# State-space tiles: direct products a tile later, modulation blocks turned by transposes, gelu steps tied behind the scan

## The chip, the cores and the metric

The kernel runs on one core of one Trainium2 chip. The metric is the device time of one execution in microseconds (us); the time before is the median of three runs. The engines are named as the profile names them: PE (TensorE's matmuls), PEld (its weight loads), DVE (VectorE), ACT (ScalarE), POOL (GpSimd) and SP (SyncE, which issues most DMAs).

## The reference

Two decoder layers over one sequence of 256 positions and 2048 channels, all in float32. Each layer has a token mixer and a SwiGLU feed-forward part, each followed by a layer norm with a scaled residual; shifts, scales and gates come from a projection of a conditioning vector. The first layer's mixer, which the change touches, is a state-space model (S5): 128 groups of 16 channels, 64 complex states in each group.

```python
def reference(x, c, ada_w, ada_b, ...):
    c_act = jax.nn.silu(c)
    for i in range(DEPTH):
        mod = c_act @ ada_w[i] + ada_b[i]
        sh_m, sc_m, gt_m, sh_f, sc_f, gt_f = [m[:, None, :] for m in jnp.split(mod, N_MOD, axis=-1)]
        h = x * (1.0 + sc_m) + sh_m
        y = s5_mixer(h, ...) if i % N_MIXERS == 0 else conv_mixer(h, ...)
        x = layer_norm(ALPHA * x + (1.0 + gt_m) * y, ln_g[i, 0], ln_b[i, 0])
        h = x * (1.0 + sc_f) + sh_f
        y = swiglu_ffn(h, ffn_w_gu[i], ffn_w_down[i])
        x = layer_norm(ALPHA * x + (1.0 + gt_f) * y, ln_g[i, 1], ln_b[i, 1])
    return x

def s5_mixer(u, ...):
    ...
    bu = jnp.einsum('btgi,gpi->btgp', u_c.astype(jnp.complex64), b_bar)
    _, h_local = lax.associative_scan(_ssm_combine, (a_elems, bu), axis=1)
    h = h_local + a_pow[None] * h0[:, None]
    y_c = jnp.real(jnp.einsum('btgp,gip->btgi', h, c_mat))
    ...
    y = jax.nn.gelu(y + d_skip.astype(f32) * u.astype(f32)).astype(u.dtype)
    vg = y @ w_glu
    return vg[..., :d] * jax.nn.sigmoid(vg[..., d:])
```

## The kernel before

The state-space part works on 16 tiles of 128 channels (eight groups), all 256 positions at once. Positions are folded in pairs, so that a scan runs over 128 steps. For tile `ct` these steps follow each other:

- `weights_in` copies the input matrices to `mb` (ACT, L396), transposes them on PE into the bank `btr` (L404) and copies that to `lz` (ACT, L405).
- `inputs` transposes x on PE into the bank `xt` (L1333, L1337), and ACT makes from it the modulated inputs `uh` and `u` and the scaled residual `X` (L940, L1345).
- `drive` multiplies `uh` by `lz` into `pin` (PE, L441), a tile of two PSUM banks with two buffers.
- `tables` prepares the rotation table `tab` (ACT L375, POOL L362) and the decay `rho` (ACT, L384).
- `scan` works on DVE: it rotates `pin` (L461, L462, L468, L469), runs one hardware scan over it (L472), and rotates back into `pc` (L461, L462) and `psn` (L459, L462). `pc` and `psn` have one buffer each.
- `weights_out` makes `dd` (the skip on a diagonal, L413) and the output matrices `mc` (L416, L417) on ACT. Nine products on PE (`bdp`, L419 and L423) give the direct block, by which an input acts on the output of its own pair, and ACT copies it to `bd` (four copies, L427).
- `read_out` adds into the bank `y`: the products of `bd` and `dd` with `u` (L484, L485), and those of `mc` with `pc` and `psn` (L495).
- `gelu` takes `y` in three steps: a square on ACT (L1352); a step on DVE (L1355) with a sigmoid on ACT (L1356); and a product on DVE to `gl` (L1360), which is then split into a high part (ACT, L1361) and a low part (POOL, L1362).

These steps are staggered. In iteration `ct` of the loop at L1412, PE issues in this order: `weights_in(ct+1)`, a modulation unit, `read_out(ct-1)`, `inputs(ct+1)`, a modulation unit, `drive(ct+1)`, the nine products of `weights_out(ct+1)`, and the rest of the modulation units. DVE does `scan(ct)` with the gelu steps of tile `ct-1`, each called at one of the places marked `between()`.

Modulation units fill PE's time: each is a DMA of 1 MB of `ada_w` to a buffer `raw` (SP's queue, L583) and four or eight matmuls with the conditioning vector repeated in 32 columns (L627). Four units make a block of 512 columns; its sums lie in the 128 partitions, as four groups of 32 equal rows. ACT copies the block to `adas` (L630). When the next unit is called, the block is first turned (`ada_turn`): four matmuls with a selecting column of `ada_sel` put the totals into columns of a bank `adat` (L635), and one DVE step adds the bias to give `mod` (L637). `plan` sets the units of a tile: 4, 4, 2, 2, then 3 in eight tiles, then 4 in the last four.

What sets the order: in the loop PE's order is the program's (`manual_schedule`). The other engines' instructions are placed by a list scheduler, which works with its own estimate of durations, and each engine then executes in that fixed order. `queue_behind` and `issue_after` add an edge: an instruction is placed on its engine behind another. PSUM banks named `aux` are shared by `btr`, `bdp`, `adat`, `xt` and `y`, three of them. After the loop the last scan and the last gelu run beside the first units of the dense stage (`s5_w_glu`).

Of the kernel before, what the change touches and what calls it, by code (L numbers as in the profile page):

```python
# [11 lines left out]
F32 = mybir.dt.float32  # L12
# [7 lines left out]
P = 128  # L20
# [135 lines left out]
class S5:  # L156
# [250 lines left out]
    def weights_out(self, ct, skip, behind):  # L407

        nc, k = self.nc, ct % 4
        qc, mb, mc = self.qm[ct // 4][1], self.mb[ct % 2], self.mc[ct % 2]  # L410
        dd = self.dd[ct % 2]
        with self.tc.issue_after(behind.ins):
            nc.scalar.mul(dd, self.ident, skip)  # L413
            for par in range(2):
                ps = slice(64 * par, 64 * par + 64)
                nc.scalar.copy(out=mc[ps, 0:4, :, par], in_=qc[ps, :, 4 * k:4 * k + 4])  # L416
                nc.scalar.activation(out=mc[ps, 4:6, :, par], in_=qc[ps, 0:3:2, 4 * k:4 * k + 4], func=AF.Copy, scale=-1.0)  # L417
        bk = self.bank("bdp")
        nc.tensor.matmul(bk[:, 0:32], dd, self.fold, start=True, stop=False)  # L419
        for r_, end in ((0, False), (1, True)):  # L420
            for p in range(4):
                r = slice(32 * p, 32 * p + 32)
                nc.tensor.matmul(  # L423
                    bk[r, 0:32], mb[:, r_, 2 * (p % 2) + p // 2, 1].rearrange("p a b -> p (a b)"), self.cols(ct, r_, p), start=False, stop=end)
        for p in range(4):
            r = slice(32 * p, 32 * p + 32)
            nc.scalar.copy(out=self.bd[ct % 2][r, r], in_=bk[r, 0:32])  # L427
# [16 lines left out]
    def scan(self, ct, pin, tab, between):  # L444

        nc, w = self.nc, self.work
        v = nc.vector
        t, rh = tab

        def turn(out, k):
            o, i = (z.rearrange("p a h r (s c) -> p (a h) r s c", s=2) for z in (out, pin))
            if k == 2:
                for r in range(2):
                    v.scalar_tensor_tensor(out=o[:, :, r, 0], in0=i[:, :, r, 0], scalar=-1.0, in1=t[:, 1, :, ::-1], op0=MUL, op1=MUL)  # L459
            else:  # L460
                v.tensor_tensor(out=o[:, :, :, 0], in0=i[:, :, :, 0], in1=bc(t[:, k, :, ::-1], 2, 2), op=MUL)  # L461
            self.end = v.tensor_tensor(out=o[:, :, :, 1], in0=i[:, :, :, 1], in1=bc(t[:, min(k, 1)], 2, 2), op=MUL)  # L462

        x1 = w.tile([P, 2, 2, 2, HALF], F32, tag="x1", name="x1")
        turn(x1, 0)
        turn(pin, 1)
        xf, pf = (z.rearrange("p a h r (s c) -> p (a h) (r s) c", s=2) for z in (x1, pin))
        v.tensor_tensor(out=pf[:, :, 0::3], in0=xf[:, :, 2:0:-1], in1=pf[:, :, 0::3], op=ADD)  # L468
        v.tensor_tensor(out=pf[:, :, 1:3], in0=xf[:, :, 3::-3], in1=pf[:, :, 1:3], op=SUB)  # L469
        between()  # L470
        z = pin.rearrange("p a h r c -> p (a h r c)")
        v.tensor_tensor_scan(out=z, data0=rh.rearrange("p q r c -> p (q r c)"), data1=z, initial=0.0, op0=MUL, op1=ADD)  # L472
        between()
        pc, psn = (w.tile([P, 2, 2, 2, HALF], F32, tag=n, name=n) for n in ("pc", "psn"))
        turn(pc, 0)
        between()
        turn(psn, 2)
        return pc, psn

# [21 lines left out]
def kernel(  # L501
# [9 lines left out]
    nc = tc.nc  # L511
# [37 lines left out]
        return v.rearrange("a (k p) -> (a k) p", p=P)  # L549

    s5 = S5(tc, const, ident, auxp, "aux", pin_ctx.enter_context(tc.tile_pool(name="pin", bufs=2, space=PSUM)))
    ada_sel = tp.tile([P, 16], F32, name="ada_sel", bufs=1)
    nc.gpsimd.tensor_copy(out=ada_sel, in_=s5.fold[:, 0:16])
    s5_prep = ExitStack()
    s5_pp = s5_prep.enter_context(tc.tile_pool(name="s5prep", bufs=1, side="right"))
    s5.load(s5_pp, s5_lam_re[0], s5_lam_im[0], s5_log_dt)
# [62 lines left out]
    def ada_block(layer, j, c0, n):  # L619

        acc = auxp.tile([P, 512], F32, tag="ada", name="ada", bufs=1)[:, :n]
        kn = 2048 // n
        for u in range(NCH // kn):
            r = load_unit(ada_w[layer], kn * u, kn, [(j * D + c0, n)])
            for k in range(kn):
                kk = kn * u + k
                nc.tensor.matmul(acc[32 * (k % 4):32 * (k % 4) + 32, :], c_rep[:, kk, :], r[:, k, :], start=kk < 4, stop=kk >= NCH - 4)  # L627
            if kk == NCH - 1:
                part = tp.tile([P, 512], F32, tag="adas", name="adas", bufs=1)[:, :n]
                nc.scalar.copy(out=part, in_=acc)  # L630
            yield
        nb, ch = n // P, c0 // P
        tr = aux("adat")[:, :nb]
        for b in range(nb):
            nc.tensor.matmul(tr[:, b:b + 1], part[:, b * P:(b + 1) * P], ada_sel[:, 0:1], start=b == 0, stop=b == nb - 1)  # L635
        with queue_behind([s5.ready]):
            nc.vector.scalar_tensor_tensor(  # L637
                out=mod[layer][:, j, ch:ch + nb], in0=tr, scalar=plus_one(j), in1=ab_col[layer][:, 16 * j + ch:16 * j + ch + nb], op0=ADD, op1=ADD)

    class AdaQueue:  # L640

# [43 lines left out]
        def add(self, layer, j, b0, k, r):  # L685
            nb = 4 - b0
            rows, n = 4 // nb, 512 * nb
            if k == 0:
                self.acc = sp_ada.tile([P, D], F32, tag="adaacc", name="adaacc")
            acc = self.acc[:, :n]  # L690
            for i in range(rows):
                kk = rows * k + i
                if kk == 0:
                    nc.vector.tensor_scalar(out=acc, in0=r[:, 0], scalar1=c_act[:, 0:1], scalar2=None, op0=MUL)
                else:
                    nc.vector.scalar_tensor_tensor(out=acc, in0=r[:, i], scalar=c_act[:, kk:kk + 1], in1=acc, op0=MUL, op1=ADD)  # L696
            if kk < NCH - 1:
                return
            h = 32 * nb

            def total():
                ps = auxp.tile([P, 512], F32, tag="ada", name="adar", bufs=1)
                for b in range(nb):
                    nc.tensor.matmul(ps[32 * b:32 * b + 32, :], ones[:, 0:32], acc[:, 512 * b:512 * b + 512], start=True, stop=True)
                part = tp.tile([P, 512], F32, tag="adas", name="adas", bufs=1)
                nc.scalar.copy(out=part[:h], in_=ps[:h])
                later.put(1, lambda: turned(part))

            def turned(part):
                tr = aux("adat")  # L710
                for b in range(4):
                    nc.tensor.transpose(tr[:, b * h:(b + 1) * h], part[:h, b * P:(b + 1) * P], ident[:h, :h])
                nc.vector.scalar_tensor_tensor(
                    out=mod[layer][:, j, 4 * b0:].rearrange("p (b c) -> p c b", c=4),
                    in0=tr[:, :4 * h].rearrange("p (c b r) -> p c b r", b=nb, r=32)[:, :, :, 0],
                    scalar=plus_one(j), in1=ab_col[layer][:, 16 * j + 4 * b0:16 * j + 16].rearrange("p (b c) -> p c b", c=4),
                    op0=ADD, op1=ADD)

            later.put(1, total)


# [625 lines left out]
    def gelu(ct, u, y):  # L1347

        vv, uu = y, u.rearrange("p (t c) -> p t c", t=2)

        def first():
            nc.scalar.activation(out=uu, in_=vv, func=AF.Square, scale=math.sqrt(0.044715))  # L1352

        def second():
            nc.vector.scalar_tensor_tensor(out=uu, in0=uu, scalar=1.0, in1=vv, op0=ADD, op1=MUL)  # L1355
            nc.scalar.activation(out=uu, in_=uu, func=AF.Sigmoid, scale=GELU_C)  # L1356

        def third():
            g = w.tile([P, SEQ], F32, tag="gl", name="gl", bufs=1)
            last = nc.vector.tensor_tensor(out=g.rearrange("p (t c) -> p t c", t=2), in0=uu, in1=vv, op=MUL)  # L1360
            nc.scalar.copy(out=hh[:, ct], in_=g)  # L1361
            nc.gpsimd.tensor_tensor(out=hl[:, ct], in0=g, in1=hh[:, ct].bitcast(F32), op=SUB)  # L1362
            return last

        return first, second, third
# [23 lines left out]
    def scan(ct, now, y):  # L1389
# [1 line left out]
        nonlocal held  # L1391
        turns = list(gelu(*held[:2], y)) if held else []

        def between():
            if turns:
                turns.pop(0)()

        held = ct, now[1], *s5.scan(ct, now[2], tabs.pop(ct), between)
        while turns:
# [2 lines left out]
    with tc.manual_schedule(engines={mybir.EngineType.PE}):  # L1402
# [9 lines left out]
        for ct in range(NCH - 1):  # L1412
            now, y = coming, None
            if (ct + 1) % 4 == 1 and ct < 12:
                load_x(ct // 4 + 1)
            s5.weights_in(ct + 1)
            n = plan[ct + 1]
            ada_units(n > 0)
            with queue_behind([] if ct else [s5.made]):
# [8 lines left out]
            s5.weights_out(ct + 1, d_col[:, ct + 1:ct + 2], last)  # L1428
            ada_units(n - 2)
            if ct == NCH - 2:  # L1430
                raws[:] = [rawp]
                more.close()
                s5.keep_ctx.close()
# [15 lines left out]
    def s5_end():  # L1449
        y = s5.read_out(*held)  # L1450
        for fn in gelu(*held[:2], y):
            last = fn()
        held_back[:] = [last]
        s5.work_ctx.close()
        s5.mats_ctx.close()
# [318 lines left out]
```

## Time and profile before

| | us |
|---|---|
| median of three runs | 2298.04 (2293.91 to 2303.72) |
| profiled execution, its time | 2298.96 |
| its span, first to last instruction | 2296.8 |
| PE busy (share of the span) | 2237.6 (97%) |
| PEld busy | 1814.5 (79%) |
| DVE busy | 1671.6 (73%) |
| ACT busy | 1019.6 (44%) |
| POOL busy | 157.2 (7%) |
| start of the scan of tile 0 | 43.41 |
| start of the scan of tile 15 | 221.87 |

A line of the timeline gives the start, the length, the engine, the source line, the operation, the tile written and the tiles read, their shapes, and how often it occurs; in brackets stands the idle time of the engine ahead of it and what ended it. PE's matmuls in float32 appear as two records each, transposes as one. A row of waits says who waited for whom, how long in total, how often, and the longest. The columns of a view of windows are the length, the busy time of PE, PEld, DVE, ACT and POOL with the number of records, the mean granted TensorE clock (1.00 is full speed), the busy share of the DMA engines and GB/s. Durations of neighbouring lines on one engine overlap a little, so distances are taken from start to start.

### The profile page before, as it was taken

To read this page: it belongs to the slowest core of one execution; us is meant where nothing else is said; L and a number is where in the kernel's file an instruction comes from. 1 tells how busy PE (TensorE), PEld (TensorE's weight loads), DVE (VectorE), ACT (ScalarE), POOL (GpSimd) and SP (SyncE) were. 2 spreads that over 40 slices of the span, in tenths; PEclk is the share of its full clock that TensorE was granted. 3 is DMA by queue.
4 is the path that set the end of the run, shared out by engine and by line. 5 is a ranking of instruction groups with operands and counts; after the bars stand their busy time and mean duration, and the time that the engine had idled before them with its cause. 6 is when DMAs were issued, how large, how long until landed. Compare 5 with 4: busy or idle time off the path is not lost.

```text
span 2296.8 us, 33538 instructions
## 1 busy us (share of the span) xinstructions
PE 2237.6 (97%) x13683; PEld 1814.5 (79%) x13683; DVE 1671.6 (73%) x1808; ACT 1019.6 (44%) x1237; POOL 157.2 (7%) x266
## 2 busy tenths in 40 slices
PE   7998999999999999999999999999999999999998
PEld 4555877988778887878898776898888888888888
DVE  8787888887777777777989788888755444545474
ACT  5665334654433333334446333656443333344343
POOL 5762000000000000000010110000000000000000
PEclk8999999999999999999999999999999999999999
DMA  9988799588999899899866774766875555555542
GB/s 333 312 288 263 267 337 356 166 307 309 323 321 324 331 317 315 312 309 328 303 209 195 213 209 160 271 218 202 289 234 191 187 192 190 183 192 191 185 166 91
DMA packets 380607, 579.48 MB, mean 252 GB/s; under 512 B 13875, under 2 KB 277939, under 8 KB 365987
## 3 DMA queue, kind: packets, MB, share of 16 engines
q1 hardware_dynamic: 379862, 576.82, 74.2%
q8 instruction: 107, 1.75, 0.3%
q0 software_dynamic: 352, 0.45, 0.1%
q14 instruction: 46, 0.38, 0.1%
q10 hardware_dynamic: 240, 0.08, 0.0%
HBM read 573.72 MB, written 3.57 MB: 251 GB/s over the span
## 4 chain that ended last, share of the span: by engine, by line
PE 80%; DVE 8%; ACT 5%; DMA 5%; issue 2%; POOL 0%; SPq 0%; DVEq 0%; ACTq 0%
PE acc L884 63%; PE acc L888 5%; DMA raw<-in_ffn_w_gu_dram 3%; DVE wlo L829 2%; PE acc L1000 2%; PE turned L900 2%; ACT whi L828 2%; PE ada L627 1%; PE y L495 1%; DMA raw<-in_s_w_glu_dram 1%; PE conv L1665 1%; DVE adaacc L696 1%; PE adat L635 1%; PE xt L1337 0%; ACT uh L940 0%
## 5 line engine op out<-in xcount | busy, mean ns | idle before, releaser
L829 DVE TENSOR_TENSOR wlo<-raw,whi 128x2048 fp32r<-128x2048 f32 x344 | 788.8, 2294 | 461.9 <-ACT whi L828 454.9
L828 ACT CAST whi<-raw 128x2048 fp32r<-128x2048 f32 x344 | 655.5, 1906 | 814.4 <-PE acc L884 426.1
L884 PE MATMUL acc<-whi,h 128*128 128x512 f32 x3648 | 892.0, 393 | 7.3 <-ACT whi L828 7.0
L884 PEld LDWEIGHTS acc<-whi,h 128*128 128x128 f32 x3648 | 679.6, 188 | 161.7 <-ACT whi L828 14.5
L884 PE MATMUL acc<-wlo,h 128*128 128x512 f32 x1824 | 461.4, 390 | 0.5 <-DVE wlo L829 0.4
L884 PEld LDWEIGHTS acc<-wlo,h 128*128 128x128 f32 x1824 | 341.8, 188 | 73.1 <-DVE wlo L829 2.2
L884 PE MATMUL acc<-whi,f 128*128 128x512 f32 x1248 | 300.9, 391 | 0.0
L696 DVE SCALAR_TENSOR_TENSOR adaacc<-rawa,c_act,adaacc 128x2048 f32<-128x2048 f32 (+1 forms) x135 | 284.5, 2107 | 0.4
L884 PEld LDWEIGHTS acc<-whi,f 128*128 128x128 f32 x1248 | 232.8, 188 | 49.5 <-ACT whi L828 1.7
L884 PE MATMUL acc<-wlo,f 128*128 128x512 f32 x624 | 156.4, 389 | 0.0
L884 PEld LDWEIGHTS acc<-wlo,f 128*128 128x128 f32 x624 | 117.1, 188 | 24.3
L1595 POOL TENSOR_TENSOR lw<-fold,wtap 128x1024 f32<-128x1024 f32 x12 | 26.3, 2196 | 1062.1 <-PE acc L888 872.8
L627 PE MATMUL ada<-raw,c_rep 128*32 128x512 f32 (+1 forms) x576 | 76.8, 634 | 2.3 <-POOL qc L324 1.6
L1233 ACT ACTIVATE fsg<-acc 128x256 f32<-128x256 f32 x84 | 31.7, 379 | 98.2 <-PE acc L884 98.2
L888 PE MATMUL acc<-h,whi 128*128 128x256 f32 x512 | 67.3, 286 | 2.8 <-DVE h L1698 2.2
L888 PEld LDWEIGHTS acc<-h,whi 128*128 128x128 f32 x512 | 63.7, 193 | 8.0 <-DVE h L1698 3.1
L1177 POOL CAST lnmh<-lno 128x2 fp32r<-128x2 f32 x1 | 0.2, 181 | 885.2 <-DVE lno L68 885.2
L1234 DVE TENSOR_TENSOR fsg<-acc,fsg 128x256 f32<-128x256 f32 x84 | 35.0, 419 | 17.2 <-ACT fsg L1233 17.2
L1665 PE MATMUL conv<-vs,lw 128*32 128x256 f32 x720 | 42.2, 380 | 0.1
L888 PE MATMUL acc<-f,whi 128*128 128x256 f32 x320 | 40.7, 284 | 0.0
L888 PEld LDWEIGHTS acc<-f,whi 128*128 128x128 f32 x320 | 39.3, 192 | 0.2
L472 DVE TENSOR_TENSOR_SCAN pin<-rho,pin 128x1024 f32<-128x1024 f32 x16 | 36.7, 2292 | 0.4
(349 smaller groups left out, 1859.1 us busy)
## 6 DMA issues: line engine op xcount, KB each, us to landing
raw<-in_ffn_w_gu_dram SPq DMA_DIRECT2D x352, 512.0 KB, 4.7
rawa<-in_ada_w_dram SPq DMA_DIRECT2D x128, 1024.0 KB, 5.6
raw<-in_ffn_w_down_dram SPq DMA_DIRECT2D x88, 1024.0 KB, 5.1
raw<-in_ada_w_dram SPq DMA_DIRECT2D x64, 1024.0 KB, 7.9
raw<-in_s_w_glu_dram SPq DMA_DIRECT2D x64, 512.0 KB, 5.9
raw<-in_cv_w_pw_dram SPq DMA_DIRECT2D x64, 512.0 KB, 5.8
raw<-in_cv_w_pw_dram SPq DMA_DIRECT2D x16, 1024.0 KB, 5.7
vs<-scr SPq DMA_DIRECT2D x40, 142.0 KB, 5.8
```

The costliest lines, as they stand in the source:

```text
L472: v.tensor_tensor_scan(out=z, data0=rh.rearrange("p q r c -> p (q r c)"), data1=z, initial=0.0, op0=MUL, op1=ADD)
L627: nc.tensor.matmul(acc[32 * (k % 4):32 * (k % 4) + 32, :], c_rep[:, kk, :], r[:, k, :], start=kk < 4, stop=kk >= NCH - 4)
L696: nc.vector.scalar_tensor_tensor(out=acc, in0=r[:, i], scalar=c_act[:, kk:kk + 1], in1=acc, op0=MUL, op1=ADD)
L828: m1 = nc.scalar.copy(out=self.hi[:, :kn], in_=r[:, :kn])
L829: m2 = nc.vector.tensor_tensor(out=self.lo[:, :kn], in0=r[:, :kn], in1=self.hi[:, :kn].bitcast(F32), op=SUB)
L884: nc.tensor.matmul(acc[bank].rearrange("p a b -> p (a b)"), x[:, bank * HALF:(bank + 1) * HALF], wt[:, k], start=first, stop=end)
L888: nc.tensor.matmul(acc[bank][:, i], wt[:, k, m * P:(m + 1) * P], x, start=first and i == 0, stop=end and i == 1)
L900: nc.tensor.transpose(b[:, o:o + HALF], u[t][:, c0 + k * P:c0 + (k + 1) * P], ident)
L1000: nc.tensor.matmul(acc[m][:, 0:EW], wt[:, k, m * P:(m + 1) * P], xx[:, 4 * u + k], start=u == 0 and n == 0, stop=u == 3 and n == len(order ...
L1233: nc.scalar.activation(out=t[:, i], in_=gv[:, 0], func=AF.Sigmoid)
L1234: nc.vector.tensor_tensor(out=t[:, i], in0=gv[:, 0], in1=t[:, i], op=MUL)
L1665: nc.tensor.matmul(acc[32 * q:32 * q + 32, :], lw[:, q, g, :], vs[:, q, 4 * g:4 * g + SEQ], start=g == 0, stop=g == n - 1)
```

## The change

Three edits.

- The direct block's nine products and four copies become a method of their own, `direct(ct)`. It is called one iteration later, behind `weights_in(ct+1)`; for tile 0 in iteration 1 ahead of `weights_in(2)`, and for tile 15 at the end of iteration 14. `dd` and `mc` are still made where they were.
- A modulation block is turned by four transposes of 128 by 128 instead of the four products with `ada_sel`, which is dropped. A DVE reduction adds the four rows that count (columns 0, 32, 64 and 96 of each transposed block) and puts the sums in the same PSUM bank; the step to `mod` reads them there. The tile `adas` gets 16 columns more, which nothing uses.
- The DVE steps of gelu get an edge each: the second step (L1355) behind the scan, the third (L1360) behind the last step to `pc`.

```diff
+    def direct(self, ct):
+
+        nc, mb, dd = self.nc, self.mb[ct % 2], self.dd[ct % 2]
         bk = self.bank("bdp")
         nc.tensor.matmul(bk[:, 0:32], dd, self.fold, start=True, stop=False)
...
-        v.tensor_tensor_scan(out=z, data0=rh.rearrange("p q r c -> p (q r c)"), data1=z, initial=0.0, op0=MUL, op1=ADD)
-        between()
+        done = v.tensor_tensor_scan(out=z, data0=rh.rearrange("p q r c -> p (q r c)"), data1=z, initial=0.0, op0=MUL, op1=ADD)
+        between(done)
         pc, psn = (w.tile([P, 2, 2, 2, HALF], F32, tag=n, name=n) for n in ("pc", "psn"))
         turn(pc, 0)
-        between()
+        between(self.end)
         turn(psn, 2)
...
-    ada_sel = tp.tile([P, 16], F32, name="ada_sel", bufs=1)
-    nc.gpsimd.tensor_copy(out=ada_sel, in_=s5.fold[:, 0:16])
...
-                part = tp.tile([P, 512], F32, tag="adas", name="adas", bufs=1)[:, :n]
+                part = tp.tile([P, 528], F32, tag="adas", name="adas", bufs=1)[:, :512][:, :n]
...
-        tr = aux("adat")[:, :nb]
+        tr = aux("adat")
         for b in range(nb):
-            nc.tensor.matmul(tr[:, b:b + 1], part[:, b * P:(b + 1) * P], ada_sel[:, 0:1], start=b == 0, stop=b == nb - 1)
+            nc.tensor.transpose(tr[:, b * P:(b + 1) * P], part[:, b * P:(b + 1) * P], ident)
+        sums = tr[:, 1:1 + nb]
         with queue_behind([s5.ready]):
-            nc.vector.scalar_tensor_tensor(
-                out=mod[layer][:, j, ch:ch + nb], in0=tr, scalar=plus_one(j), in1=ab_col[layer][:, 16 * j + ch:16 * j + ch + nb], op0=ADD, op1=ADD)
+            nc.vector.tensor_reduce(
+                out=sums, in_=tr[:, :n].rearrange("p (b q r) -> p b q r", q=4, r=32)[:, :, :, 0], axis=mybir.AxisListType.X, op=ADD)
+        nc.vector.scalar_tensor_tensor(
+            out=mod[layer][:, j, ch:ch + nb], in0=sums, scalar=plus_one(j), in1=ab_col[layer][:, 16 * j + ch:16 * j + ch + nb], op0=ADD, op1=ADD)
...
-        def second():
-            nc.vector.scalar_tensor_tensor(out=uu, in0=uu, scalar=1.0, in1=vv, op0=ADD, op1=MUL)
+        def second(behind):
+            with queue_behind(behind):
+                nc.vector.scalar_tensor_tensor(out=uu, in0=uu, scalar=1.0, in1=vv, op0=ADD, op1=MUL)
             nc.scalar.activation(out=uu, in_=uu, func=AF.Sigmoid, scale=GELU_C)
 
-        def third():
+        def third(behind):
             g = w.tile([P, SEQ], F32, tag="gl", name="gl", bufs=1)
-            last = nc.vector.tensor_tensor(out=g.rearrange("p (t c) -> p t c", t=2), in0=uu, in1=vv, op=MUL)
+            with queue_behind(behind):
+                last = nc.vector.tensor_tensor(out=g.rearrange("p (t c) -> p t c", t=2), in0=uu, in1=vv, op=MUL)
...
+            if ct == 1:
+                s5.direct(0)
             s5.weights_in(ct + 1)
+            if ct:
+                s5.direct(ct)
             n = plan[ct + 1]
             ada_units(n > 0)
...
             if ct == NCH - 2:
+                s5.direct(ct + 1)
```

More of the change, by code (lines that the diff above doesn't have):

```diff
@@ L409, in weights_out @@
         nc, k = self.nc, ct % 4
-        qc, mb, mc = self.qm[ct // 4][1], self.mb[ct % 2], self.mc[ct % 2]
+        qc, mc = self.qm[ct // 4][1], self.mc[ct % 2]
         dd = self.dd[ct % 2]
@@ L704, in total @@
                     nc.tensor.matmul(ps[32 * b:32 * b + 32, :], ones[:, 0:32], acc[:, 512 * b:512 * b + 512], start=True, stop=True)
-                part = tp.tile([P, 512], F32, tag="adas", name="adas", bufs=1)
+                part = tp.tile([P, 528], F32, tag="adas", name="adas", bufs=1)[:, :512]
                 nc.scalar.copy(out=part[:h], in_=ps[:h])
@@ L1349, in gelu, with first @@
         vv, uu = y, u.rearrange("p (t c) -> p t c", t=2)
-        def first():
+        def first(behind):
             nc.scalar.activation(out=uu, in_=vv, func=AF.Square, scale=math.sqrt(0.044715))
-        def second():
-            nc.vector.scalar_tensor_tensor(out=uu, in0=uu, scalar=1.0, in1=vv, op0=ADD, op1=MUL)
+        def second(behind):
+            with queue_behind(behind):
+                nc.vector.scalar_tensor_tensor(out=uu, in0=uu, scalar=1.0, in1=vv, op0=ADD, op1=MUL)
             nc.scalar.activation(out=uu, in_=uu, func=AF.Sigmoid, scale=GELU_C)
-        def third():
+        def third(behind):
             g = w.tile([P, SEQ], F32, tag="gl", name="gl", bufs=1)
-            last = nc.vector.tensor_tensor(out=g.rearrange("p (t c) -> p t c", t=2), in0=uu, in1=vv, op=MUL)
+            with queue_behind(behind):
+                last = nc.vector.tensor_tensor(out=g.rearrange("p (t c) -> p t c", t=2), in0=uu, in1=vv, op=MUL)
             nc.scalar.copy(out=hh[:, ct], in_=g)
@@ L1392, in scan, with between @@
         turns = list(gelu(*held[:2], y)) if held else []
-        def between():
+        def between(*behind):
             if turns:
-                turns.pop(0)()
+                turns.pop(0)(behind)
         held = ct, now[1], *s5.scan(ct, now[2], tabs.pop(ct), between)
@@ L1451, in s5_end @@
         for fn in gelu(*held[:2], y):
-            last = fn()
+            last = fn(())
         held_back[:] = [last]
```

## The prediction

> **What bounds the kernel now.** The diff touches only the state-space stage, so I first looked for where that stage lies. The scan (L472), one for each of 16 tiles, begins at 43.41 us for tile 0 and at 221.87 us for tile 15. I cut this stretch at the scans' starts in the view of windows (the columns are length, then busy time of PE, PEld, DVE, ACT, POOL, then the granted clock, the DMA share and GB/s), and asked for the waits of DVE and PE over the 13 intervals from scan 2 to scan 15.
>
> ```profile
> 71.84:221.87 150.03, 133.62 (x1961) 80.34 (x1959) 124.61 (x194) 99.83 (x284) 82.55 (x155) 0.92 0.83 280
> ...
> 104.76:116.49 11.73, 10.76 (x156) 6.43 (x152) 9.59 (x15) 7.20 (x22) 10.90 (x27) 0.85 0.91 305
> ...
> 139.86:149.50 9.64, 9.64 (x162) 5.50 (x156) 9.40 (x16) 7.47 (x22) 6.57 (x13) 1.00 0.94 330
> ...
> 195.83:209.15 13.32, 11.91 (x172) 6.83 (x164) 9.74 (x15) 7.05 (x20) 3.54 (x6) 0.88 0.65 220
> ```
>
> 150.03 us for 13 tiles is 11.54 us a tile, and 124.61 us of DVE is 9.59. The tile from 139.86 took 9.64 us with DVE busy for 9.40: a tile can go at VectorE's own pace. Others with the same DVE work take 11.73 or 13.32, at a lower granted clock. So the stage alternates between VectorE and TensorE, and what it loses stands in the waits (us in total, times, longest):
>
> ```profile
> DVE mod L637 <- PE adat L635: 7.2, 7, 1.6
> DVE gl L1360 <- ACT u L1356: 5.8, 7, 1.8
> DVE u L1355 <- ACT u L1352: 5.6, 5, 1.9
> DVE pc L461 <- PE y L495: 2.1, 2, 1.2
> DVE x L461 <- PE pin L441: 1.9, 2, 0.9
> ...
> PE adat L635 <- ACT adas L630: 6.3, 5, 1.6
> PE bdp L423 <- ACT mc L416: 5.5, 11, 0.5
> PE bdp L419 <- ACT dd L413: 1.7, 4, 0.5
> ```
>
> The five DVE rows add up to 22.6 us: DVE without them would need 127.4 us. That is the most the change could take out here. DMA is not the bound: its queue waits for TensorE to give buffers back.
>
> ```profile
> SPq L583 <- PE ada L627: 176.1, 52, 26.0
> ```
>
> The 13 tiles moved 280 GB/s, and the tile from 139.86 moved 330. The same bytes in 137 us need 280 x 150/137 = 307 GB/s, still below that.
>
> **Part 1, gelu steps tied behind the scan.** Nothing is added; two VectorE steps and the sigmoid between them get an order. In the interval from 104.76 VectorE stood still ahead of the first of them, with the scan's last preparation (L469) and the scan behind it:
>
> ```profile
> 112.83 0.69 DVE L468 TENSOR_TENSOR pin<-x,pin 128x512 f32<-128x512 f32 x1
> 115.43 0.42 DVE L1355 SCALAR_TENSOR_TENSOR u<-u,y 128x256 f32<-128x256 f32 x1 [1.90 <-ACT u L1352]
> 115.77 0.69 DVE L469 TENSOR_TENSOR pin<-x,pin 128x512 f32<-128x512 f32 x1
> 116.49 2.29 DVE L472 TENSOR_TENSOR_SCAN pin<-rho,pin 128x1024 f32<-128x1024 f32 x1
> 118.82 0.69 DVE L461 TENSOR_TENSOR pc<-pin,tab 128x512 f32<-128x512 f32 x1
> 119.43 0.68 DVE L462 TENSOR_TENSOR pc<-pin,tab 128x512 f32<-128x512 f32 x1
> 120.03 0.41 DVE L1360 TENSOR_TENSOR gl<-u,y 128x256 f32<-128x256 f32 x1
> ...
> 113.89 1.06 PE L495 MATMUL y<-psn,mc 128*32 128x128 f32 x32
> ```
>
> Behind the scan, the step comes later by L469 (0.72 from start to start) and the scan (2.33): 3.05 us, more than the longest wait of 1.9. So the row of 5.6 us goes whole: -5.6. What is late next is pc, which shares its buffer with the y product; its last records began at 113.89 and took 1.06, so it had ended at 114.95, when pc would start at 118.82 - 1.90 = 116.92 and not wait.
>
> The second step (gl) needs the sigmoid. From L1355's start to gl's place there would be 0.33 for L1355 itself and 1.21 us for the two pc steps; 0.41 plus the sigmoid's 0.42 fits. But ScalarE is in order:
>
> ```profile
> 177.09 0.42 ACT L1356 ACTIVATE u<-u 128x256 f32<-128x256 f32 x1
> 177.42 0.72 ACT L427 COPY bd<-bdp 32x32 f32<-32x32 f32 x4
> ...
> 180.54 0.58 ACT L630 COPY adas<-ada 128x512 f32<-128x512 f32 x1
> ...
> 129.95 0.42 DVE L1360 TENSOR_TENSOR gl<-u,y 128x256 f32<-128x256 f32 x1 [0.72 <-ACT u L1356]
> ...
> 172.90 0.42 DVE L1355 SCALAR_TENSOR_TENSOR u<-u,y 128x256 f32<-128x256 f32 x1 [0.25 <-ACT u L1352]
> ...
> 177.61 0.42 DVE L1360 TENSOR_TENSOR gl<-u,y 128x256 f32<-128x256 f32 x1 [1.83 <-ACT u L1356]
> ...
> 217.88 0.42 DVE L1360 TENSOR_TENSOR gl<-u,y 128x256 f32<-128x256 f32 x1 [0.79 <-ACT u L1356]
> ```
>
> L1355 had run at 172.90, and the sigmoid of that tile came only at 177.09, in its place in ScalarE's order. That order can stay. Bounds of this term: all 5.8 us gone, or the longest wait of 1.83 in all 13 tiles, 23.8 - 5.8 = +18.0. I take -2.3: three waits (the first 0.72 at 129.95, the last 0.79 at 217.88, and another 0.79 between), where gl followed a late L1355 with little between them, and leave the other four to ScalarE's order.
>
> **Part 2, direct blocks at the next tile's beginning.** Moved are nine products (18 records, L419 and L423) on PE and the four copies to bd on ACT; no DMA, and nothing of SP's or POOL's queue. On PE they pass the last modulation units and the transposes to btr; on ACT they leave the place ahead of rho and adas shown above, 0.72 us. Now PE reaches them before mc is there:
>
> ```profile
> 118.74 0.33 PE L423 MATMUL bdp<-mc,mb 128*32 128x32 f32 x16 [0.50 <-ACT mc L416]
> 118.89 1.04 PE L627 MATMUL ada<-raw,c_rep 128*32 128x512 f32 x8
> 119.86 0.66 PE L404 MATMUL btr<-ident,mb 128*128 128x128 f32 x4
> 121.57 1.05 PE L635 MATMUL adat<-ada_sel,adas 128*128 128x1 f32 x8 [1.05 <-ACT adas L630]
> ...
> 106.95 0.33 PE L423 MATMUL bdp<-mc,mb 128*32 128x32 f32 x16 [0.49 <-ACT mc L416]
> ...
> 110.20 1.93 PE L627 MATMUL ada<-raw,c_rep 128*32 128x512 f32 x8
> ...
> 208.24 1.94 PE L627 MATMUL ada<-raw,c_rep 128*32 128x512 f32 x8
> ```
>
> A modulation unit (0.97 us from the start of one at 118.89 to btr at 119.86) and btr later, mc is long written, so the PE waits for dd and mc, 5.5 + 1.7 = 7.2 us, go. Then the direct products (0.33 for L423's eight; two more for L419) stand between btr and the turn of the modulation block and fill part of its wait for adas. PE time alone earns nothing in tiles that VectorE paces; it shortens what VectorE waits for. Two rows do: pc and x, 2.1 + 1.9 = 4.0 us, all in the last two intervals, with four units a tile. Of the tile from 195.83, PE's 0.50 at mc and the low clock go: the unit at 208.24 takes 1.94 against 1.04, 0.9 more. Two such tiles with about 1.4 to 1.5: -3.0 (bounds 0 and -4.0).
>
> The clock is a cost in itself. Some 3 us after the gap of 0.49 us ahead of 106.95, PE's unit at 110.20 took 1.93 instead of 1.04, and the interval from 104.76 has 0.85. The Trainium skill ("TensorE: Matmul & The Clock Gate", Part 1, HAM oscillation) says that the clock drops once PE idles for a whole window of some 3.4 us; by that, removing gaps of half a microsecond would give no clock back, and this term would be 2 x 0.5 = -1.0 rather than -3.0. The trace speaks against it: PE was busy 10.76 of that interval's 11.73 us, so no gap came near 3.4 us, and still the clock fell; the interval with PE busy throughout (from 139.86) stands at 1.00.
>
> **Part 3, the turn by transposes.** Eight records of 1.05 us become four like btr's 0.66, 0.39 less for each of the 10 turns between scans 2 and 15. ScalarE's copy to adas stands up to 0.72 us sooner without the bd copies, so the turn ends about 1 us sooner in the tiles where mod is waited for 1.0 to 1.6 us. VectorE's place for mod isn't fixed by the change, and VectorE too arrives sooner. Bounds of the row of 7.2: gone, or all still there. I take half, -3.6. Added is one reduction for each block, 16 elements in and 4 out of each partition. No such row exists; nearest is mod itself:
>
> ```profile
> 108.31 0.16 DVE L637 SCALAR_TENSOR_TENSOR mod<-adat,adab 128x4 f32<-128x4 f32 x1
> 108.39 0.42 DVE L1360 TENSOR_TENSOR gl<-u,y 128x256 f32<-128x256 f32 x1
> ```
>
> It took 0.08 us from start to start and 0.16 in all. The reduction reads four times its elements; I take the middle, 0.12 x 10 = +1.2 (bounds 0.8 and 1.6). The ada_sel copy on POOL before the stage and the padding of part cost nothing: POOL is busy 82.55 of the 13 tiles' 150.03 us, and the padded columns are never touched.
>
> **Start and end.** From scan 1 to scan 2 y(0) is late, and direct(0) and direct(1) still stand ahead of it, now beside the transposes; their wait for mc goes (0.50 in the row at 118.74), and y(0) gets a wait for bd's copies (0.72 in the row at 177.42): 0, bounds -2 and +2. Behind scan 15 the dense stage is paced by its weights; one turn and the last gelu there: 0.
>
> **Sum**: -5.6 - 2.3 - 3.0 - 3.6 + 1.2 = -13.3 us. The profiled execution took 2298.96 (span 2296.8), 0.92 above the median of 2298.04. 2298.96 - 13.3 = 2285.7; rounded, 2286. The stage would then run at (150.03 - 13.3)/13 = 10.5 us a tile.
>
> **Rivals.**
> *The PSUM bank.* Three banks serve btr, bdp, adat, y and xt; y holds one until gl. The new order puts btr, bdp and adat into one run, while y is held. For it:
>
> ```profile
> 109.19 0.68 PEld L404 LDWEIGHTS btr<-ident,mb 128*128 128x128 f32 x4 [0.84 <-DVE gl L1360]
> 109.19 1.08 PE L404 MATMUL btr<-ident,mb 128*128 128x128 f32 x4
> ```
>
> PE now comes about 1 us sooner to that place, so I estimate the wait at 0.84 to 1.8 us in the ten tiles with a turn. Against it: bank choice isn't in the trace, and PE has room in three-unit tiles. It would eat the terms of mod, pc and x (-6.6): 2292.
>
> *The transposes lower the clock.* As a mechanism of this kernel: each turn brings a slow stretch, costing 0.89 for a unit (1.93 against 1.04) and 0.42 for btr (1.08 against 0.66), 1.3 x 10 = 13 us of PE, partly the stretches it has already. Against it: 139.86 to 149.50, with four transposes, stands at 1.00. The terms of mod, pc and x would go here too: 2292. The same page of the Trainium skill (Part 4, PE-mode transpose) says that transposes don't count as busy for the clock gate, which is this rival; no run here shows it yet.
>
> *ScalarE paces gl; the other side.* If gl, now always directly behind pc, waits in every tile for a sigmoid that stands behind dd and mc, its term is up to +18.0 instead of -2.3, and the sum -11.0 + 18.0 = +7.0: 2306. It is slower than before from an average wait of (11.0 + 5.8)/13 = 1.3 us a tile. Against it: gl's place further back isn't forbidden, and of 13 tiles 7 have a wait now, 5.8/7 = 0.8 us on average.
>
> *All waits go*: -5.6 - 5.8 - 4.0 - 7.2 + 0.8 = -21.8: 2277.
>
> **Chances and range.** Forecast 0.52, bank 0.15, clock 0.10, ScalarE 0.10, all waits 0.13. What a measurement of this kernel can tell from no change is about 0.5%, 11.5 us: the border lies at 2286.5, in the middle of the forecast's own range (2281 to 2293). So faster is 0.13 and a little over half of 0.52, 0.42 in all; same is the rest of the forecast, both middle rivals and the mild half of ScalarE's, 0.52; slower 0.06. The range runs from 2275 to 2300, which leaves out the far end of ScalarE's case and little else.
>
> **What would show it.** Right: L1355 behind every scan with no wait of over 0.3 us ahead of it; bdp without a wait for dd or mc; adat at about 0.66; granted clock near 1.0 in most tiles; 10 to 10.8 us from scan to scan. Wrong: a row of PE waiting for gl or for bd; gl or the new reduction waiting over 0.8 us a tile; intervals of 11.5 us still.

## The result and the profile after

The changed kernel takes 2275.61 us (median of four runs, 2274.40 to 2277.76) against 2295.97 us before (four runs): a ratio of 0.9907, 95% interval 0.9880 to 0.9933. It is 20.4 us faster, where 12 were forecast and the likeliest outcome (0.52) was one that a measurement can't tell from no change; the time lies at the fast end of the range. One of the five executions of the kernel with the turn alone (`turn_only`, below) took 5458.29 us, more than twice the others, and is left out of its ratio.

The gain lies in the state-space stage. The view of windows of the changed kernel, cut at the starts of its scans (now L476) as before: the sum from scan 2 to scan 15, four tiles with three units, then two with four.

```profile
71.86:201.85 129.99, 117.08 (x1903) 71.20 (x1895) 123.99 (x203) 98.69 (x283) 81.13 (x151) 0.98 0.92 320
...
91.11:100.87 9.76, 9.76 (x168) 5.83 (x162) 9.52 (x16) 8.75 (x27) 7.24 (x14) 1.00 1.02 360
...
120.34:130.15 9.81, 9.81 (x172) 6.06 (x168) 9.47 (x14) 8.42 (x25) 6.01 (x11) 1.00 0.86 293
...
139.91:149.68 9.77, 8.02 (x114) 5.28 (x114) 9.53 (x16) 6.08 (x18) 9.22 (x24) 0.83 0.98 347
149.68:160.66 10.98, 10.01 (x178) 6.20 (x173) 9.62 (x17) 8.02 (x23) 7.79 (x13) 1.00 0.78 265
160.66:171.00 10.34, 9.22 (x138) 5.33 (x134) 9.54 (x16) 7.53 (x22) 2.77 (x5) 1.00 0.88 304
...
180.84:191.20 10.36, 9.63 (x160) 5.71 (x160) 9.67 (x17) 6.83 (x20) 2.74 (x5) 1.00 0.93 346
```

The 13 tiles take 129.99 us instead of 150.03, so 20.0 us of the 22.1 by which the spans differ (2274.7 against 2296.8). Scan 2 begins where it did, at 71.86. Tiles with up to three units now run at 9.6 to 9.8 us, but for one of 10.98, with VectorE busy for about 9.5; those with four units need 9.8 to 10.65. The granted clock is 0.98 instead of 0.92. The waits of VectorE and TensorE in the same stretch:

```profile
DVE gl L1367 <- ACT u L1362: 3.1, 4, 1.2
...
PE adat L637 <- ACT adas L632: 5.0, 7, 1.1
...
PE bdp L423 <- DVE mod L642: 1.9, 1, 1.9
PE bdp L423 <- DVE gl L1367: 1.6, 1, 1.6
...
PE bdp L427 <- ACT mc L416: 0.5, 1, 0.5
```

Of VectorE's five rows before (22.6 us) one is left. TensorE's waits for dd and mc fell from 7.2 to 0.5. The waits of bdp for mod and gl are those of the bank rival. The first of them:

```profile
103.07 0.66 PE L404 MATMUL btr<-ident,mb 128*128 128x128 f32 x4
105.63 0.38 PE L423 MATMUL bdp<-fold,dd 128*128 128x32 f32 x2 [1.91 <-DVE mod L642]
...
103.08 0.41 DVE L1361 SCALAR_TENSOR_TENSOR u<-u,y 128x256 f32<-128x256 f32 x1
...
104.92 0.17 DVE L640 TENSOR_REDUCE adat<-adat 128x4 f32<-128x16 f32 x1
105.00 0.41 DVE L463 SCALAR_TENSOR_TENSOR psn<-pin,tab 128x256 f32<-128x256 f32 x1
105.34 0.15 DVE L642 SCALAR_TENSOR_TENSOR mod<-adat,adab 128x4 f32<-128x4 f32 x1
```

PE stood for 1.91 us until mod was written; the trace doesn't name banks, but a bank that adat still held explains it. That tile still took 9.77 us (100.87 to 110.64). The reduction takes 0.17 us, and 0.08 from start to start. The second, in the tile from 139.91, was not free:

```profile
144.51 0.41 PE L423 MATMUL bdp<-fold,dd 128*128 128x32 f32 x2 [1.57 <-DVE gl L1367]
...
146.88 1.94 PE L499 MATMUL y<-pc,mc 128*32 128x128 f32 x32
148.58 1.59 PE L499 MATMUL y<-psn,mc 128*32 128x128 f32 x32
...
154.67 0.42 DVE L1367 TENSOR_TENSOR gl<-u,y 128x256 f32<-128x256 f32 x1 [1.18 <-ACT u L1362]
```

Behind the wait of 1.57 us the clock fell, and the products of y took 1.94 and 1.59 us where they take 1.08 and 1.06 otherwise. ScalarE, which had waited for y, came late to the sigmoid, VectorE waited 1.18 us for it, and that tile is the one of 10.98.

### The profile page after: what moved, and what is told of

It is laid out like the page before. It is cut to its first block, busy times and chain, and to the rows that moved or that the text cites. A ratio compares the mean times of both kernels' runs of the same rounds, so it can differ in the third digit from the quotient of the medians.

```text
span 2274.7 us, 33445 instructions
## 1 busy us (share of the span) xinstructions
PE 2221.7 (98%) x13619; PEld 1804.2 (79%) x13619; DVE 1671.7 (73%) x1826; ACT 1018.8 (45%) x1237; POOL 157.0 (7%) x265
## 4 chain that ended last, share of the span: by engine, by line
PE 79%; DVE 10%; DMA 4%; ACT 4%; issue 2%; SPq 0%; POOL 0%; DVEq 0%; ACTq 0%
PE acc L889 65%; PE acc L893 6%; DVE wlo L834 3%; DMA raw<-in_ffn_w_gu_dram 3%; ACT whi L833 2%; PE acc L1005 2%; PE turned L905 2%; PE conv L1677 1%; DVE adaacc L701 1%; PE y L499 1%; DMA raw<-in_s_w_glu_dram 1%; PE ada L629 1%; DMA raw<-in_ada_w_dram 1%; DVE pin L476 1%; PE adar L709 0%
## 5 line engine op out<-in xcount | busy, mean ns | idle before, releaser
L629 PE MATMUL ada<-raw,c_rep 128*32 128x512 f32 (+1 forms) x576 | 71.3, 592 | 6.0 <-DMA raw<-in_ada_w_dram 3.6
L476 DVE TENSOR_TENSOR_SCAN pin<-rho,pin 128x1024 f32<-128x1024 f32 x16 | 36.7, 2294 | 0.5
```

The lines of the kernel that those rows point to most:

```text
L476: done = v.tensor_tensor_scan(out=z, data0=rh.rearrange("p q r c -> p (q r c)"), data1=z, initial=0.0, op0=MUL, op1=ADD)
```

## The experiments

**Each part alone, and the whole without the direct part.** The edits are the hunks of the diff: `gelu_only` has the ties, `direct_only` the direct method and its calls, `turn_only` the transposes with the reduction, `no_direct` the first and the last of these.

> The kernel before with only the gelu steps tied behind the scan. Theory of separate rows (each part of the change takes out the wait rows that it touches): L1355's row of 5.6 us and 2.3 us of gl's go, about -8 us. Rival of a common cause (TensorE comes late because of its own gaps and the clock that they cost, and every VectorE wait is that lateness seen at another place): the wait only moves to mod, pc or x; -4 us or less, and the granted clock in the 13 tiles stays near 0.92.

> The kernel before with only the direct blocks a tile later. Separate rows: TensorE's waits for dd and mc go, VectorE's waits for pc and x (4.0 us) shrink by 3: -3 us. Common cause: the granted clock rises towards 1.0, TensorE is earlier everywhere, and the rows of mod, L1355, gl, pc and x all shrink: -12 us or more.

> The kernel before with only the modulation blocks turned by transposes. Separate rows: half of mod's row goes and the reduction costs 1.2: -2 to -3 us. Common cause: TensorE's gaps at mc stay, so does the clock; -1 to -4 us. The rival that transposes lower the clock: granted clock below 0.92 in the 13 tiles, 0 or slower.

> The changed kernel with the direct blocks where they were before (gelu tied, turns by transposes). Separate rows: 3 us slower than the changed kernel, so about -17 against before. Common cause: most of the gain is lost, -6 us or less against before, with TensorE's waits for dd and mc and a granted clock near 0.92 back.

Ratios to before: gelu alone 0.9996 (0.9982 to 1.0011); direct alone 0.9942 (0.9918 to 0.9965); turn alone 0.9924 (0.9891 to 0.9956); gelu and turn 0.9924 (0.9899 to 0.9950). In the gelu kernel, VectorE's waits between scans 2 and 15:

```profile
DVE gl L1362 <- ACT u L1357: 9.7, 8, 2.1
DVE mod L637 <- PE adat L635: 8.9, 7, 1.6
DVE pc L461 <- PE y L495: 2.2, 2, 1.2
DVE x L461 <- PE pin L441: 1.9, 2, 0.9
```

L1355's row is gone, as meant, and the sum is 22.7 us, as before: gl has 3.9 more and mod 1.7 more. The wait moved and nothing was gained. The windows of direct alone with VectorE's waits, then those of turn alone with TensorE's waits:

```profile
72.95:209.24 136.29, 125.34 (x1943) 78.63 (x1935) 123.51 (x194) 98.90 (x283) 80.87 (x151) 0.95 0.88 304
...
DVE u L1359 <- ACT u L1356: 4.0, 2, 2.4
DVE gl L1364 <- ACT u L1360: 2.5, 4, 0.8
DVE x L465 <- PE pin L445: 2.2, 3, 0.9
DVE pc L465 <- PE y L499: 1.0, 1, 1.0
```

```profile
70.62:206.62 136.00, 120.28 (x1921) 70.90 (x1919) 124.58 (x203) 99.39 (x284) 82.38 (x156) 0.99 0.91 311
```

```profile
PE bdp L423 <- ACT mc L416: 5.5, 11, 0.5
...
PE bdp L419 <- ACT dd L413: 1.6, 4, 0.5
```

Either part by itself takes 14 us out of the stage. For the direct part the theory of a common cause had said 12 or more; for the turn no theory had said more than 4. The direct part empties mod's row, which it doesn't touch. In turn alone TensorE still stands for dd and mc as long as before, and yet its clock is 0.99. So those gaps by themselves don't lower the clock; with the one-column products beside them it is 0.92, and without the gaps but with the products (direct alone) 0.95. The rival that transposes lower the clock falls. In `no_direct` the theory of separate rows had the right number, -17 us (measured, by the ratio: -17.5). The common cause, as it was written down for that run, failed: the gaps are back, the clock stays at 0.99, and most of the gain stays too.

What 0.92 consists of shows when the kernel before is cut finer. The clock is 0.50 in seven stretches of 3.41 us, whole multiples of 3.41 us apart, and 1.00 between them. One of them, with the stretch ahead of it:

```profile
105.86:109.27 3.41, 2.73 (x35) 1.72 (x36) 3.38 (x7) 3.32 (x12) 3.05 (x11) 1.00 0.91 330
109.28:112.69 3.41, 3.41 (x15) 1.42 (x16) 3.27 (x6) 1.86 (x5) 3.18 (x7) 0.50 0.66 201
...
106.95 0.33 PE L423 MATMUL bdp<-mc,mb 128*32 128x32 f32 x16 [0.49 <-ACT mc L416]
107.22 1.05 PE L635 MATMUL adat<-ada_sel,adas 128*128 128x1 f32 x8
```

Ahead of each of the seven stands such a stretch with gaps of 0.68 to 1.64 us and a turn by one-column products (about 1.05 us) together. In the rest of the stage it stayed at 1.00 behind a turn with gaps of at most 0.22 us (three times), and behind gaps of up to 1.4 us without a turn. Longer gaps did lower it without a turn: 2.6 us at the stage's end are followed by one more such stretch, just outside it. So the seven fall where gaps and turn meet, and either part of the change takes away much of one of them.

**What of the turn counts: how it streams, or how long it takes?** First, the kernel before with 96 selecting columns instead of one (the 32 columns of `fold` three times; only the first of each 96 results is read):

```diff
-    ada_sel = tp.tile([P, 16], F32, name="ada_sel", bufs=1)
...
+    ada_sel = tp.tile([P, 96], F32, name="ada_sel", bufs=1)
+    for q in range(3):
+        nc.gpsimd.tensor_copy(out=ada_sel[:, 32 * q:32 * q + 32], in_=s5.fold)
...
-            nc.tensor.matmul(tr[:, b:b + 1], part[:, b * P:(b + 1) * P], ada_sel[:, 0:1], ...)
+            nc.tensor.matmul(tr[:, b * P:b * P + 96], part[:, b * P:(b + 1) * P], ada_sel, ...)
```

Then the changed kernel with products added behind the transposes, one column wide or 128:

```diff
+        for b in range(nb if layer == 0 and (j, c0) != (3, 512) else 0):
+            nc.tensor.matmul(acc[:, b:b + 1], part[:, b * P:(b + 1) * P], ident[:, 0:1], start=True, stop=True)
```

```diff
+        for b in range(nb if layer == 0 and (j, c0) != (3, 512) else 0):
+            nc.tensor.matmul(acc[:, 0:P], part[:, b * P:(b + 1) * P], ident, start=True, stop=True)
```

> The kernel before, its turn still by products with the selecting column, but with that column repeated to 96, so that each product streams 96 columns instead of 1 (the same count of records, no transposes, no reduction on VectorE, PE's turn not shorter than 1.05 us). Theory N: the one-column products leave TensorE idle in the eyes of its clock, and the low clock (0.92 in the 13 tiles) is what the transposes took away; then the clock rises to 0.97 or more here too and the time falls by 10 us or more. Rival S (shorter): the transposes gain because they take 0.66 us instead of 1.05; then this kernel is as slow as before, within 3 us. Rival O (order): the reduction gave VectorE's two steps another place; then this kernel is as slow as before too.

> The changed kernel with, behind each turn's transposes, the one-column products of before again, into a bank that nothing reads any more (11 of 12 blocks; no result changes). Theory N: the clock falls back under 0.95 and 8 us or more of the gain is lost. Rival S: TensorE has room beside VectorE, 1.0 us more a turn costs at most the tiles with four units, 0 to 4 us, and the clock stays at 0.98.

> The same with products of 128 columns instead of one, as many records and about 1.3 us of PE a turn. Theory N: the clock stays at 0.98 and the loss is smaller than that of the one-column products, 0 to 4 us. Rival S: the loss is as large as theirs or larger, since PE's time is longer.

`wide_turn` is at 0.9974 (0.9959 to 0.9989), some 6 us faster than before. `narrow_added` is at 0.9928 (0.9913 to 0.9943) and `wide_added` at 0.9933 (0.9912 to 0.9953): by these ratios they are 5 and 6 us slower than the changed kernel (the intervals overlap with its own), and in the profiled stage 8.4 and 11.4. The windows, in this order, and the added products of the last two:

```profile
69.34:215.21 145.87, 128.28 (x1961) 78.36 (x1959) 124.42 (x194) 100.02 (x284) 82.43 (x155) 0.96 0.86 293
```

```profile
73.93:212.30 138.37, 128.72 (x1983) 81.97 (x1975) 124.60 (x204) 98.61 (x282) 81.05 (x151) 0.96 0.86 296
...
L639 PE MATMUL ada<-ident,adas 128*128 128x1 f32 x80 | 9.5, 240 | 0.0
```

```profile
71.35:212.73 141.38, 129.55 (x1995) 82.82 (x1988) 129.25 (x205) 100.70 (x283) 85.15 (x157) 0.99 0.90 306
...
L639 PE MATMUL ada<-ident,adas 128*128 128x128 f32 x80 | 10.6, 275 | 0.0
...
208.21 4.61 DVE L836 TENSOR_TENSOR wlo<-raw,whi 128x2048 fp32r<-128x2048 f32 x2
```

The last line is a step of the dense stage, which in `wide_added` stands ahead of scan 15 and in the others behind it. Its 4.6 us don't belong to the products: up to scan 14 the stage is longer than the changed kernel's by 7.5 us with the narrow products and by 6.1 with the wide ones.

The clock does follow the width: 9.5 us of one-column products bring it to 0.96, 10.6 us of wide ones leave it at 0.99, with as many weight loads beside them (PEld 9.7 us in both). The three slow stretches of `narrow_added` each follow gaps of 0.8 to 1.0 us and such products together; the only one of `wide_added` follows a wait of 3.1 us for the dense stage. The clocks of whole executions bear out `wide_turn`: 0.990 to 0.993 in 8, against 0.984 to 0.988 in 11 of the kernel before. Those of the added products overlap (0.989 to 0.990 and 0.989 to 0.994), so this pair rests on one profile each.

But as a full account of the time, theory N failed: by the ratios the wide products cost as much as the narrow ones, and the wide turn gained 6 us and not 10. So did rival S, by which TensorE had room: ten turns of 1.0 us more cost 8 us of the profiled stage. Both TensorE's own time and the clock count.

**Two attempts to go further.** One makes dd and mc behind the sigmoid on ACT, the other the copy to rho behind the copy to adas:

```diff
-            s5.weights_out(ct + 1, d_col[:, ct + 1:ct + 2], last)
+            if ct in (0, NCH - 2):
+                s5.weights_out(ct + 1, d_col[:, ct + 1:ct + 2], last)
...
+            if 0 < ct < NCH - 2:
+                s5.weights_out(ct + 1, d_col[:, ct + 1:ct + 2], sigmoid[0])
```

```diff
-                tabs[ct + 1] = s5.tables(ct + 1, [last])
+                tabs[ct + 1] = s5.tables(ct + 1, [last], ct > 0)
...
             ada_units(n - 2)
+            if ct:
+                s5.decay(ct + 1, [last, *copied])
```

> The changed kernel with dd and mc made on ACT behind the sigmoid of the same tile instead of ahead of it (13 tiles). Theory: gl's 3.1 us of waits are ACT's order and go, 2 to 3 us faster than the changed kernel, about 0.990 against before. Rival: mc then comes later than bdp wants it, TensorE waits there again, and nothing or less than nothing is gained.

> The changed kernel with ACT's copy to rho (1.02 us) placed behind the copy to adas, so that TensorE's wait for adas ahead of the turn (5.0 us, seven times up to 1.1) shrinks. Theory P: the four-unit tiles, 10.3 to 10.7 us now, fall to about 9.8; -2 to -3 us against the changed kernel. Rival V: VectorE with its 9.65 us a tile paces those too and gl's waits stay: within 1 us of the changed kernel.

`sigmoid_first` is at 0.9900 (0.9882 to 0.9917) and `rho_later` at 0.9915 (0.9900 to 0.9930): neither differs from the changed kernel beyond the intervals. In the first, TensorE's waits for mc came back, as its rival said, and gl's were not smaller:

```profile
DVE gl L1367 <- ACT u L1362: 3.3, 4, 1.5
...
PE bdp L427 <- ACT mc L416: 2.8, 4, 1.3
PE bdp L423 <- ACT dd L413: 1.6, 3, 1.0
```

In the second, the last three four-unit tiles took 10.07 to 10.08 us, where the changed kernel has 9.84, 10.36 and 10.65, but the wait for adas fell only from 5.0 to 3.9 us, and tiles before them rose (10.91 and 10.47 us where the changed kernel has 9.62 and 9.70).

**The whole without gelu, and without the turn.**

> The changed kernel without the gelu ties (direct blocks a tile later, turns by transposes). Theory P (TensorE's path sets the tile: its work, plus its waits, plus what the low clock costs; VectorE's waits are the shadow of that): TensorE's path is the changed kernel's, the stage between scans 2 and 15 takes 130 to 133 us, within 3 us of the changed kernel. Theory R (each part takes out its own VectorE rows): L1355's waits come back, 5 us or more slower than the changed kernel.

> The changed kernel with the one-column turn of before (gelu tied, direct blocks a tile later). Theory P: 4 us of PE for ten turns and about 4 us of clock (0.95 instead of 0.98) come back, +6 to +9 us against the changed kernel, near the kernel with the direct blocks alone. Theory R: mod's half row less the reduction, +2.4 us.

Without the gelu ties: 0.9898 (0.9884 to 0.9913), as fast as the changed kernel. L1355's waits did not come back as 5 us, but as 1.3:

```profile
71.47:200.95 129.48, 117.00 (x1903) 71.13 (x1895) 123.94 (x203) 98.53 (x283) 80.95 (x151) 0.98 0.93 322
...
DVE gl L1365 <- ACT u L1361: 1.3, 2, 0.8
DVE u L1360 <- ACT u L1357: 1.3, 2, 1.1
```

Without the transposes: 0.9936 (0.9920 to 0.9953), the stage 136.88 us, within 0.6 us of that with the direct part alone. Theory P, TensorE's path, held in both (129.48 us lies just under its 130 to 133).

**More work for VectorE.** gl's product twice in each tile of the changed kernel:

```diff
-                last = nc.vector.tensor_tensor(out=g.rearrange("p (t c) -> p t c", t=2), in0=uu, in1=vv, op=MUL)
+                for _ in range(2):
+                    last = nc.vector.tensor_tensor(out=g.rearrange("p (t c) -> p t c", t=2), in0=uu, in1=vv, op=MUL)
```

> The changed kernel with gl's product on VectorE done twice in each tile (the same result written twice), 0.33 us more of VectorE a tile from start to start, 4.3 us in the 13 tiles. Theory D (with TensorE's path shortened, VectorE paces the tiles): the stage takes 130 + 4.3 us, and the tiles of 9.6 to 9.8 us become 9.95 to 10.1. Rival: TensorE still paces most tiles; the stage stays within 1.5 us of 130.0.

0.9926 (0.9908 to 0.9944). Tiles that took 9.6 to 9.8 us take 10.0 to 10.1, by the whole 0.33:

```profile
134.31:144.34 10.03, 9.72 (x169) 6.03 (x165) 9.79 (x16) 7.98 (x24) 7.52 (x14) 1.00 1.00 341
144.34:154.44 10.10, 9.43 (x156) 5.63 (x160) 9.86 (x18) 7.75 (x24) 9.55 (x25) 1.00 0.94 337
154.44:164.82 10.38, 7.47 (x78) 4.27 (x74) 10.01 (x17) 5.27 (x16) 7.68 (x12) 0.68 0.70 238
164.82:177.74 12.92, 12.77 (x226) 8.03 (x222) 10.04 (x17) 8.20 (x24) 2.80 (x5) 0.99 0.77 280
```

The stage grew by 8.7 us (138.74), twice what was forecast: some other tiles lost 2 us more, with waits of up to 2.9 us for lz on ACT and a clock of 0.68 in one of them. The clock's mean fell to 0.94, 8.3 us lost in the stage instead of 2.6. Why ACT's copy came so late there was not followed up. In the changed kernel VectorE sets the pace of most three-unit tiles, and TensorE is close behind it.

## Why the prediction was wrong

The mechanism was named (the stage alternates between VectorE and TensorE), and the sum was made on the wrong engine. It priced VectorE's rows of waits part by part, and took a share of each. The runs show that these rows don't belong to single parts: tying the gelu steps emptied one row and filled others by as much, while the direct part alone brought the five rows from 22.6 to 9.7 us, and the turn alone to 8.8. They fit one cause for the most part: VectorE waiting, directly or by way of ScalarE, for a late TensorE. What a part is worth is what it takes off TensorE's path. That the sum came as near as it did is luck: 7.9 of its 13.3 us stood for the ties, which gained nothing, and parts 2 and 3, put at 5.4 together, brought the whole gain.

An account in TensorE's terms, from one profile of each kernel: the stage from scan 2 to scan 15; the clock's loss, (1 - granted clock) x length, from two digits of the clock and so good to 0.7 us; the waits for dd and mc; the busy time of the turn, with the products added to it; and what is left.

| kernel | stage | clock's loss | waits for dd, mc | turn on PE | rest |
|---|---|---|---|---|---|
| before | 150.0 | 12.0 | 7.2 | 10.7 | 120.1 |
| gelu only | 149.7 | 12.0 | 6.9 | 10.6 | 120.2 |
| direct only | 136.3 | 6.8 | 0.5 | 10.5 | 118.5 |
| turn only | 136.0 | 1.4 | 7.1 | 6.6 | 120.9 |
| gelu and turn | 136.1 | 1.4 | 7.1 | 7.0 | 120.6 |
| gelu and direct | 136.9 | 6.8 | 0.5 | 10.6 | 119.0 |
| direct and turn | 129.5 | 2.6 | 0.5 | 6.5 | 119.9 |
| all three | 130.0 | 2.6 | 0.5 | 6.6 | 120.3 |
| wide turn | 145.9 | 5.8 | 7.0 | 13.9 | 119.2 |
| sigmoid first | 132.8 | 1.3 | 4.8 | 7.0 | 119.7 |
| rho later | 131.1 | 2.6 | 0.5 | 7.0 | 121.0 |
| narrow added | 138.4 | 5.5 | 0.5 | 16.1 | 116.3 |
| wide added | 141.4 | 1.4 | 0.5 | 17.2 | 122.3 |
| vector added | 138.7 | 8.3 | 0.5 | 7.0 | 122.9 |

In the first eleven kernels the rest stays within 118.5 to 121.0 us while the stage varies by 20. It is an account made afterwards, and its terms overlap; but it fits the wide turn as well, which differs from before by little but TensorE's work. It fits the last three less well. With the products added to the changed kernel the rest is smaller (117.7 for the wide ones without the 4.6 us of the dense stage), so some of that work cost no time; with more work for VectorE it is larger.

Point by point, by the prediction's steps:

- *Part 1, -5.6 and -2.3.* Failed: 0 alone (149.71 against 150.03 us), 0 on top of the turn (136.06 against 136.00) and 0 on top of both others (129.99 against 129.48). The step "the row of 5.6 us goes whole" was right of the row and wrong of the time. The check for what is late next looked at pc alone; mod and gl were next, and gl's row grew by 3.9 us where 2.3 less were forecast.
- *Part 2, -3.0.* The row of 7.2 us on PE went as forecast. "PE time alone earns nothing in tiles that VectorE paces" was the step that failed: alone the part takes 13.7 us out of the stage, on top of the turn 6.1 to 6.5. Removing the gaps of half a microsecond gave back 5.2 us of clock in the stage (12.0 to 6.8); the part had counted 0.9 in each of two tiles.
- *Part 3, -3.6 + 1.2.* The lengths were right: 6.6 us for ten turns against 10.7, the reduction 0.08 us from start to start. The size was not: 14.0 us alone, 6.8 to 6.9 on top of the direct part. Missing was the clock. The prediction laid its loss on the gaps at mc and gave the turn none of it.
- *The clock.* 12 us of the stage lay in it, and the prediction had the row (0.92) and never multiplied it out. The tile that it compared with, from 139.86 at 1.00, has neither a gap nor a turn inside (the turn before it starts at 138.69), so it couldn't tell the two apart. The Trainium skill ("TensorE: Matmul & The Clock Gate", Part 1, "A second HAM failure mode") tells of short idles between groups of matmuls that make the clock swing. The kernel before agrees, with 0.92 where no wait of TensorE was over 1.64 us but one of 2.6 at the stage's end. The runs show one thing more: the idles for dd and mc alone left 0.99 (turn only), and products of one column act much like further idle time. The Trainium skill also says, in the same page's Part 4 ("PE-mode transpose"), that a transpose doesn't count as busy in the same way. The runs speak against it here: 0.92 rose to 0.99 when 6.6 us of transposes took the place of 10.7 us of products. How far a transpose counts is not shown, since the turn became shorter too.
- *The rivals.* "All waits go" (2277) is nearly what happened, and had a chance of 0.13. The bank's waits are there (3.5 us); one cost nothing visible, the other stands ahead of a slow stretch and the tile of 10.98 us. ScalarE's pace is left in gl's four waits, 3.1 us.
- *DMA.* 320 GB/s against the 307 that the sum needed. The row of 176.1 us that the prediction shows for its queue is of the whole execution; in the 13 tiles these waits for TensorE fell from 129.5 to 108.4 us. The one row of waits that VectorE has left is for ScalarE.

Direct alone and turn alone each gain 14 us, but together only 20. By the table most of the missing 7.7 us is the clock: its loss falls by 5.2 and 10.6 us alone but by 9.4 together, since each part takes away one half of the same pairs of gaps and one-column products. What stays open is the rest. VectorE's own 124 us, with the small steps between its instructions, is a floor that the two together reach, and the last run fits that, but how much each tile lost to it was not separated.

## What to carry to other kernels

Where two engines hand work to each other in turn, the rows of waits on one are the shadow of the other's path: add up that other path (its work at full clock, its own waits, the clock's loss) before giving each row to a part of the change, and don't add rows that can move into one another. Multiply the granted clock out, (1 - clock) x length, as a term of its own. When an edit only orders the steps of an engine that is waiting anyway, expect the wait to move. Before two stages are compared, see that they hold the same instructions: a step of the next stage made one of them 4.6 us longer.

## What the hardware showed

The granted clock of 0.92 was not an even slowdown: it was 0.50 in seven stretches of 3.41 us and 1.00 between them. Each followed a stretch of 3.41 us in which TensorE had gaps of 0.68 to 1.64 us and about 1 us of products that stream one column.

Such products lower TensorE's clock almost like idling: 9.5 us of them, spread over ten turns in 138 us, go with a clock of 0.96, and 10.6 us of products with 128 columns with 0.99 (one profile each). Gaps of half a microsecond, 7.1 us in all, beside transposes in place of those products left it at 0.99.
